# A hybrid decoder layer with 32 experts: another order of the expert steps, the last three of them scattered by products, the residual in the second step

## The chip, the cores and the metric

One Trainium2 chip; the kernel runs on 1 of its cores. The metric is the device time of one execution in microseconds (us). A core has a matmul engine (PE, with its weight loads PEld), a vector engine (DVE), a scalar engine (ACT), GpSimd (POOL) and SyncE (SP), which issues DMA transfers; ACT and POOL can issue transfers too. All transfers run on the same 16 DMA engines.

## The reference

One decoder layer on 512 tokens of 1024 values: attention in a window and a gated mixing stage, then a mixture of experts, each stage followed by a layer norm. The part that the change touches is the mixture:

```python
def routed_experts(x, w_router, b_router, w_gate_up, b_gate_up, w_down, b_down):
    top_val, top_idx = lax.top_k(logits, TOP_K)          # 4 of 32 experts for each token
    gates = jax.nn.softmax(top_val, axis=-1)
...
        h = clamped_swiglu(xb @ w_gate_up[e] + b_gate_up[e])
        y = (h @ w_down[e] + b_down[e]) * g[:, None]
        return acc.at[tok].add(y), None
...
h = layer_norm(DEEPNORM_ALPHA * h + ffn, ln2_g[l], ln2_b[l])
```

Each expert has 8 MB of gate and up weights and 4 MB of down weights, float32, so the 32 experts are 384 loads of 1 MB.

## The kernel before

The first part (to 240 us) is the attention and mixing stage, the router and the sort of the experts by the number of their tokens. Then the expert loop runs in steps, listed by the string `PLAN` (line 77). A letter is an expert: N and L are experts with up to 128 token places, X with up to 192, S with up to 64. A step is one word: `SS` is a pair of small experts that share the 128 rows of a tile and multiply at full float32 on two halves of the matmul array; `L` is one expert whose weights are first split by ACT (line 279) and DVE (line 280) into a high and a low part, three fast products for each block; `XS` is an expert of 192 places with a small one beside it, 128 rows twice, so it needs the products of two steps.

A step has an up phase (U; A and B for the two halves of XS) and a down phase (D0 and D1). The order is: up of step i, then down of step i-1, then up of step i+1; where step i is XS, the down of step i-1 lies between A and B. So every stretch below can be named by its phases: 4A, 3D, 4B, 5U, 4D and so on. Weights stream in that order. SP issues one load of 1 MB at a time (lines 293, 296, 299) into a ring of 11 buffers (`NRING_A`, `NRING_B`, `NRING_C`: 3 + 5 + 3); a buffer is free again when PE has used it, in an L step when ACT and DVE have split it. A phase of a step takes: SS up 16 loads, SS down 8, L up 8, L down 4, XS A, B and down 8 each.

Side work is written as generators that are moved on by `pump`, one piece between two groups of products: first `urgent` (the activation), then `later` (the output of a step), then the list `side` in its order, each entry when it is due. `prep` gathers the tokens of a coming step (POOL, line 1399), `prep_t` transposes them. At the end of an up phase all of `side` but the scatters is drained.

What an expert yields goes one of two ways. Up to step `LATE` - 1, `rows_out` (from line 1671) scales the result on ACT and writes it to DRAM as rows (`yd`, line 1686, issued by ACT, 0.5 MB for 128 rows). From step `LATE` on, `output` splits the result into two parts in two `sg` tiles (ACT line 1662, DVE line 1664) and `scatter` brings it to its tokens with 16 products (line 1414) and 8 additions (line 1416). The rows come back with `combine`: 16 gathers by POOL (line 1734) of 128 rows of 4 KB each, into tiles that are no longer needed; `combined` adds them to the residual stream (16 additions, line 1743). `combine` is put on `side` by `outputs(LATE - 1)`, `combined` at the end of the down phase of `LATE`. `residual` (8 products of line 1368, 8 additions of line 1371) starts the stream with the scaled input and the down biases; it runs in step 0.

`ending` (from line 1868) drains what is left on `side`, does the last half of the last down phase with loads by column halves (line 1892), places the last pair by products (line 1884) and normalises. In `side`, a scatter is put at the head; the additions of line 1743 to a token tile come after the scatter's additions to it.

```python
    seq = [(0, "A"), (0, "B"), (0, "D0"), (0, "D1")]
    for i in range(1, NS):
        down = [(i - 1, "D0"), (i - 1, "D1")] if i > 1 else []
        seq += [(i, "A")] + down + [(i, "B")] if wide(i) else [(i, "U")] + down
```

Of the kernel before, what the change touches and what calls it, by code (L numbers as in the profile page):

```python
# [73 lines left out]
R2L = R2 - R2H  # L74
PIF = 3.1415925

PLAN = "N SS L SS XS SS L L SS L L SS XS SS L L SS L L SS SS"


@with_exitstack  # L80
def kernel(ctx: ExitStack, tc: tile.TileContext, x, pos, gb_in, w_in, b_in, sinks,
                      gn_g, gn_b, w_sT, b_sT, w_out, b_out, ln1_g, ln1_b, w_router, b_router,
                      w_gu, b_gu, w_dn, b_dn, ln2_g, ln2_b, out, plan=PLAN):
    nc = tc.nc
# [22 lines left out]
    def ps_m():  # L107
        return ps[0].tile([P, 512], F32, name="misc", bufs=2)
# [105 lines left out]
    NS = len(steps)  # L214
# [19 lines left out]
        return [(steps[i][1].index(r), slice(q * n, q * n + n)) for q, (r, _) in enumerate(u)]  # L234


    LATE = NS - 2
    room = lambda r: P if r == 0 else 192 if r <= nx else P if r < nx + nl else 64
    late_ranks = [r for _, rs in steps[LATE:] for r in rs]
    first_row = [sum(room(q) for q in range(r) if q not in late_ranks) for r in range(E + 1)]  # L240
# [97 lines left out]
    with ExitStack() as pc:  # L338
# [667 lines left out]
        Q, L = {}, {}  # L1006
# [288 lines left out]
    def drain(g):  # L1295
        for _ in g:
            pass
# [21 lines left out]
    def tables():  # L1319
        pg = ps_m()  # L1320
        for t in range(T):
            nc.tensor.transpose(pg[:, t * P:(t + 1) * P], tabf[:, t].rearrange("p a e -> p (a e)"), ident)
        nc.vector.tensor_copy(trt, pg)
        yield
        pg = ps_m()
        for t in range(T):
            nc.tensor.matmul(pg[:, t * 3 * E:(t + 1) * 3 * E], lhsT=trt[:, t * P:(t + 1) * P],
                             rhs=pm3.rearrange("p a e -> p (a e)"), start=True, stop=True)
        pv = pg[:, 0:3 * T * E].rearrange("p (t j e) -> p j t e", j=3, t=T)
        nc.vector.tensor_copy(vpos, pv[:, 2])  # L1330
        for j in range(2):
            nc.vector.tensor_copy(aux[:, :, :, 1 + j], pv[:, j])
        yield

        capr = mw.tile([P, E], F32, name="capr", bufs=1)
        nc.gpsimd.memset(capr, 64.0)
        nc.gpsimd.memset(capr[:, 0:1 + nx + nl - 1], 128.0)
        if nx:
            nc.gpsimd.memset(capr[:, 1:1 + nx], 192.0)
        gover = mw.tile([P, T, E], F32, name="hT", bufs=HTB)  # L1340
        nc.vector.tensor_tensor(gover, vpos, capr[:, None, :].to_broadcast([P, T, E]), op=OP.is_gt)
        ovs = mw.tile([P, E], F32, name="capr2", bufs=1)
        nc.vector.reduce_sum(ovs, gover.rearrange("p t e -> p e t"), axis=AX.X)
        pg = ps_m()
        nc.tensor.matmul(pg[0:1, 0:E], lhsT=onec, rhs=ovs, start=True, stop=True)
        nc.vector.tensor_copy(over[:, 0:E], pg[0:1, 0:E])
        ovt = mw.tile([1, 1], F32, name="ovt", bufs=1)
        nc.vector.reduce_sum(ovt, pg[0:1, 0:E], axis=AX.X)
        nc.vector.tensor_copy(over[:, E:E + 1], ovt)
        gsum = rt.tile([P, T, E], F32, name="oh")  # L1350
        nc.gpsimd.tensor_add(gsum, aux.bitcast(F32)[:, :, :, 1], aux.bitcast(F32)[:, :, :, 2])
        nc.gpsimd.tensor_mul(gover, gover, gsum)
        nc.gpsimd.dma_start(out=god, in_=gover)
        yield
# [2 lines left out]
    for j in range(3):  # L1357
        nc.scalar.dma_start(out=braw[j * E:(j + 1) * E], in_=b_dn[0])

    def residual():  # L1360

        bdn = msplit.tile([P, 2, 512], F32R, name="hi").rearrange("p a b -> p (a b)")[0:3 * E]
        nc.scalar.copy(out=bdn, in_=braw)
        nc.vector.tensor_sub(bdn[E:E2], braw[E:E2], bdn[E:E2])
        for t in range(T):
            for c in range(2):
                pg = ps_m()
                nc.tensor.matmul(pg, lhsT=trt[0:3 * E, t * P:(t + 1) * P], rhs=bdn[:, c * 512:(c + 1) * 512],
                                 start=True, stop=True)
                h = hn[:, t, c * 512:(c + 1) * 512]  # L1370
                nc.vector.scalar_tensor_tensor(h, h, ALPHA, pg, op0=OP.mult, op1=OP.add)
                yield
# [46 lines left out]
    side = []  # L1419
# [3 lines left out]
    urgent, later = [], []  # L1423
# [49 lines left out]
    def slots0():  # L1473

        pa0 = ps_m()
        for t in range(T):
            nc.tensor.matmul(pa0[:, 0:2], lhsT=oh0[:, t], rhs=aux0[:, t], start=t == 0, stop=t == T - 1)
        SL[u0] = mw.tile([P, 4], F32, name="sl", bufs=6 + AHEAD)
        nc.vector.tensor_copy(SL[u0][:, 0:2], pa0[:, 0:2])
        yield  # L1480
# [3 lines left out]
    zrow = mw.tile([P, 2, 512], F32, name="y")  # L1484
    nc.gpsimd.memset(zrow[0:1], 0.0)
    nc.gpsimd.dma_start(out=yd[first_row[E]:first_row[E] + 1], in_=zrow[0:1].rearrange("p c j -> p (c j)"))
    side += [[slots0(), 2], [tables(), 0], [residual(), 0]]
    state = {}

    def begin(i):  # L1490
# [175 lines left out]
    def y_tile(u):  # L1666
        settle(1)
        YH[u] = [mw.tile([P, 2, 512], F32R, name="sg") for _ in range(2)]
        return YH[u]

    def rows_out(u, a):

        y = mw.tile([P, 2, 512], F32, name="y")
        gcol = SL[u][:, 1:2]
        for c in range(2):
            nc.scalar.activation(y[:, c], a[:, c], AF.Copy, scale=gcol)  # L1676
            yield
        n = P // len(u)
        if len(u) == 2 and u[0][1] == u[1][1] == 0:
            blocks = [(u[0], P)]  # L1680
        else:
            blocks = [(ro, n) for ro in u]
        p = 0
        for (r, off), m in blocks:
            row = first_row[r] + off
            nc.scalar.dma_start(out=yd[row:row + m], in_=y[p:p + m].rearrange("p c j -> p (c j)"))
            p += m
# [34 lines left out]
    def combine():  # L1722

        for n in range(4 * T):
            t, j = divmod(n, 4)
            if n < 4:
                g = mw.tile([P, KT, P], F32, name="xT", bufs=XTB).rearrange("p k s -> p (k s)")
            elif n < 6:
                g = mw.tile([P, D], F32, name="xg", bufs=AHEAD)
            elif n < 8:  # L1730
                g = mw.tile([P, 2, 512], F32, name="y").rearrange("p c j -> p (c j)")
            else:
                g = msplit.tile([P, 2, 512], F32, name="hi" if n % 2 else "lo").rearrange("p c j -> p (c j)")
            nc.gpsimd.indirect_dma_start(out=g, out_offset=None, in_=yd,
                                         in_offset=bass.IndirectOffsetOnAxis(ap=yrow[:, t, j:j + 1], axis=0))
            gathered.append((t, g))
            yield
# [3 lines left out]
    def combined():  # L1741
        for t, g in gathered:
            nc.vector.tensor_add(hn[:, t], hn[:, t], g)
            yield

    def outputs(i):
        if i < LATE:
            for u, a in zip(state[i]["us"], state[i]["dn"]):
                yield from rows_out(u, a)
                yield  # L1750
            if i == LATE - 1:
                side.append([combine(), 0])
            return
        for u, a in zip(state[i]["us"], state[i]["dn"]):
            y = y_tile(u)
            for c in range(2):
                yield from output(u, a[:, c:c + 1], y, slice(c, c + 1))
                yield
            scat.append([scatter(u), 0])
            side.insert(0, scat[-1])  # L1760
# [149 lines left out]
    with in_order():  # L1910
        before_ = None
        for i, ph in seq:
            if ph in ("U", "A"):
                begin(i)
                plan_prep(i)
            if i == NS - 1 and ph == "D1":
                break
            if ph in ("U", "A", "B") and before_ and before_[1] == "D1" and not wide(before_[0]):
                flush(urgent)
            elif ph != "D1":  # L1920
                flush()
            if ph == "U":
                phase_up(i)
            elif ph in ("A", "B"):
                phase_half(i, int(ph == "B"))
            else:
                phase_down(i, int(ph == "D1"))
            before_ = i, ph
            if i == 0:
                flush()  # L1930
            if i == LATE - 2 and ph in ("U", "A"):
                side.append([combine_rows(), 0])
            if (ph == "U" or ph == "B" and i or ph == "D1" and not i) and i < NS - 1:
                for ent in [e for e in side if e not in scat]:
                    side.remove(ent)
                    drain(ent[0])
            if ph == "D1":
                later.append(outputs(i))
                if i == LATE:
                    side.append([combined(), 0])  # L1940
                state.pop(i - 1, None)
        flush()
    ending()
# [112 lines left out]
```

## Time and profile before

| | us |
|---|---|
| device time, median of 3 runs | 1352.46 (1348.05 to 1354.04) |
| device time of the profiled execution | 1352.4 |
| its span, first to last instruction | 1350.2 |
| attention, mixing, router | 0 to 240 |
| expert loop | 240 to 1305 |
| last additions, last placing, layer norm, store | 1305 to 1350 |
| PE busy, share of the span | 91% |
| DVE busy | 47% |
| ACT busy | 32% |
| POOL busy | 14% |
| moved by DMA | 454.89 MB |

The profile is read by stretches, since its shares are means over stages with different limits. A stretch in which the transfers run at some 420 GB/s is limited by them; one in which PE is busy throughout and the transfers run slower is limited by PE.

### The profile page before, as it was taken

Reading aid. Unit: us, or ns where it says so; the run is one execution under the profiler, and the core shown is the slowest. Engines: PE = TensorE matmul, PEld = TensorE weight load, DVE = VectorE, ACT = ScalarE, POOL = GpSimd, SP = SyncE. Lnnn points to the kernel's source line nnn. Section 1 sums busy time; section 2 is a strip of 40 time slices with the busy share of each in tenths; the row PEclk is TensorE's granted clock in tenths of the full one; section 3 lists DMA queues with packets and bytes.
Section 4 is the critical chain, followed back from the end, with each engine's and each line's share of the span. In section 5 each row is a group of like instructions: output and inputs, shape, how many; then the busy total and the mean of one; then the engine's idle time right before and its main releaser. Section 6 shows DMA issues by size and latency. Waiting matters only on the chain.

```text
span 1350.2 us, 15317 instructions
## 1 busy us (share of the span) xinstructions
PE 1235.1 (91%) x5416; PEld 693.0 (51%) x5417; DVE 632.3 (47%) x1125; ACT 431.1 (32%) x623; POOL 194.9 (14%) x269
## 2 busy tenths in 40 slices
PE   5789899999998999999999999999999999997762
PEld 4767778444545333467476635333665477442220
DVE  7747767514404012268286632022565578330176
ACT  3335443103303101347174422101544356230002
POOL 5634735100001000000000010000000000003004
PEclk8889999999998999999999999999999999998895
DMA  7210185489999899999999999999999999999951
GB/s 248 79 63 32 63 270 189 152 309 420 420 421 413 314 415 415 379 422 419 378 420 421 420 419 416 361 403 421 389 420 377 403 421 422 417 421 418 417 205 65
DMA packets 85080, 454.89 MB, mean 337 GB/s; under 512 B 10813, under 2 KB 11861, under 8 KB 41476
## 3 DMA queue, kind: packets, MB, share of 16 engines
q1 hardware_dynamic: 75508, 423.76, 78.0%
q0 software_dynamic: 5536, 16.58, 3.2%
q10 hardware_dynamic: 3952, 13.51, 2.6%
q8 instruction: 44, 0.72, 0.2%
q14 instruction: 40, 0.33, 0.1%
HBM read 441.96 MB, written 15.27 MB: 339 GB/s over the span
## 4 chain that ended last, share of the span: by engine, by line
PE 73%; DMA 12%; DVE 9%; ACT 2%; issue 2%; POOL 1%; SPq 0%; ACTq 0%; POOLq 0%; DVEq 0%; another core or an unknown queue 0%
PE acc L1471 36%; PE acc L1465 7%; PE acc L1464 7%; PE acc L1467 7%; DMA raw<-in_w_dn_dram 7%; DMA raw<-in_w_gu_dram 5%; PE accA L427 2%; PE accA L428 2%; PE accA L429 2%; PE misc L1527 2%; DVE lo L280 1%; PE misc L1287 1%; ACT hi L279 1%; PE acc L1583 1%; PE misc L1386 1%
## 5 line engine op out<-in xcount | busy, mean ns | idle before, releaser
L1471 PE MATMUL acc<-raw,xT 128*64 128x512 f32 (+1 forms) x1600 | 414.5, 603 | 9.0 <-DMA raw<-in_w_gu_dram 6.6
L280 DVE TENSOR_TENSOR lo<-raw,hi 128x1024 fp32r<-128x1024 f32 x216 | 255.8, 1222 | 158.6 <-ACT hi L279 157.6
L1471 PEld LDWEIGHTS acc<-raw,xT 128*64 128x64 f32 (+1 forms) x1600 | 135.1, 144 | 237.7 <-issue 219.4
L279 ACT CAST hi<-raw 128x1024 fp32r<-128x1024 f32 x216 | 218.0, 1047 | 117.4 <-DMA raw<-in_w_gu_dram 42.1
L1471 PE MATMUL acc<-raw,hT 128*64 128x512 f32 (+1 forms) x768 | 199.1, 606 | 12.6 <-DMA raw<-in_w_dn_dram 11.8
L1399 POOL DMA_INDIRECT xg<-h1d,idx x22 | 23.9, 1085 | 827.7 <-DVE sl L1396 294.5
L1471 PEld LDWEIGHTS acc<-raw,hT 128*64 128x64 f32 (+1 forms) x768 | 65.8, 145 | 138.8 <-issue 118.6
L1464 PE MATMUL acc<-hi,xT 128*128 128x512 f32 x288 | 117.5, 408 | 0.0
L1465 PE MATMUL acc<-lo,xT 128*128 128x512 f32 x288 | 113.9, 396 | 0.0
L1467 PE MATMUL acc<-hi,xT 128*128 128x512 f32 x288 | 90.6, 396 | 0.0
L427 PE MATMUL accA<-hi,tT 128*128 128x512 f32 x152 | 66.4, 437 | 1.3 <-ACT tT L465 1.3
L1541 ACT ACTIVATE sg<-sg 128x512 f32<-128x512 f32 x38 | 24.0, 631 | 132.9 <-DVE sg L1540 132.9
L1464 PE MATMUL acc<-hi,hT 128*128 128x512 f32 x144 | 61.9, 430 | 4.0 <-ACT hi L279 4.0
L1465 PE MATMUL acc<-lo,hT 128*128 128x512 f32 x144 | 61.4, 427 | 4.0 <-DVE lo L280 4.0
L1392 DVE COPY sl<-misc 64x4 f32<-64x4 f32 (+1 forms) x33 | 5.3, 160 | 126.0 <-PE misc L1386 125.8
L428 PE MATMUL accA<-lo,tT 128*128 128x512 f32 x152 | 62.7, 413 | 0.0
L429 PE MATMUL accA<-hi,tT 128*128 128x512 f32 x152 | 62.3, 410 | 0.0
L1464 PEld LDWEIGHTS acc<-hi,xT 128*128 128x128 f32 x288 | 54.3, 189 | 14.2 <-issue 2.8
L1467 PEld LDWEIGHTS acc<-hi,xT 128*128 128x128 f32 x288 | 54.0, 188 | 13.0
L1465 PEld LDWEIGHTS acc<-lo,xT 128*128 128x128 f32 x288 | 54.2, 188 | 11.3
L1676 ACT ACTIVATE y<-acc,sl 128x512 f32<-128x512 f32 x42 | 27.2, 683 | 94.3 <-PE acc L1471 58.5
L1531 ACT COPY hT<-misc 128x512 f32<-128x512 f32 x28 | 16.4, 586 | 116.0 <-PE misc L1527 115.2
(409 smaller groups left out, 1390.6 us busy)
## 6 DMA issues: line engine op xcount, KB each, us to landing
raw<-in_w_gu_dram SPq DMA_DIRECT2D x248, 1024.0 KB, 14.0
raw<-in_w_dn_dram SPq DMA_DIRECT2D x124, 1024.0 KB, 14.9
yd<-y ACTq DMA_DIRECT2D x19, 512.0 KB, 8.0
raw<-in_w_gu_dram SPq DMA_DIRECT2D x16, 512.0 KB, 9.0
raw<-in_w_in_dram SPq DMA_DIRECT2D x7, 1024.0 KB, 13.3
raw<-in_w_out_dram SPq DMA_DIRECT2D x4, 1024.0 KB, 4.9
raw<-in_w_dn_dram SPq DMA_DIRECT2D x8, 512.0 KB, 23.9
hn<-in_x_dram SPq DMA_DIRECT2D x4, 512.0 KB, 10.9
```

The lines of the kernel that those rows point to most:

```text
L279: nc.scalar.copy(out=hi, in_=w.raw[:, 2 * h:2 * h + 2])
L280: nc.vector.tensor_sub(lo, w.raw[:, 2 * h:2 * h + 2], hi)
L427: nc.tensor.matmul(o, lhsT=a, rhs=hi, start=first, stop=False)
L428: nc.tensor.matmul(o, lhsT=a, rhs=lo, start=False, stop=False)
L429: nc.tensor.matmul(o, lhsT=b, rhs=hi, start=False, stop=last)
L1464: nc.tensor.matmul(outs[g], lhsT=lhs[0], rhs=hi[:, g], start=first, stop=False)
L1465: nc.tensor.matmul(outs[g], lhsT=lhs[0], rhs=lo[:, g], start=False, stop=False)
L1467: nc.tensor.matmul(outs[g], lhsT=lhs[1], rhs=hi[:, g], start=False, stop=last)
L1471: nc.tensor.matmul(outs[g][cs], lhsT=lhs[0][:, cs], rhs=ws[m].raw[:, 2 * q + g], start=first, stop=last)
L1527: nc.tensor.transpose(pt[:, j * P:(j + 1) * P], pick(act, j), ident)
L1541: nc.scalar.activation(g[:, 0], g[:, 0], AF.Gelu_apprx_sigmoid)
L1676: nc.scalar.activation(y[:, c], a[:, c], AF.Copy, scale=gcol)
```

## The change

Four edits. The plan has the same letters in another order: steps 5 to 20 were `SS L L SS L L SS XS SS L L SS L L SS SS` and become `L SS L L SS XS L L SS L L SS L SS SS SS`. `LATE` becomes `NS - 3`: the steps 18, 19 and 20 are scattered by products and step 17 is the last to write rows. `combine` is put on `side` behind the up phase of step `LATE + 1`, ahead of the down phase of step 18, and `combined` ahead of the output of step 18. `residual` is cut in two: `table_down` (the split of the down biases) stays in step 0, the products and additions are put on `side` at the end of step 0 and run in the up phase of step 1.

```diff
--- before.py
+++ after.py
@@ -74,7 +74,7 @@
 R2L = R2 - R2H
 PIF = 3.1415925
 
-PLAN = "N SS L SS XS SS L L SS L L SS XS SS L L SS L L SS SS"
+PLAN = "N SS L SS XS L SS L L SS XS L L SS L L SS L SS SS SS"
 
 
 @with_exitstack
@@ -234,7 +234,7 @@
         return [(steps[i][1].index(r), slice(q * n, q * n + n)) for q, (r, _) in enumerate(u)]
 
 
-    LATE = NS - 2
+    LATE = NS - 3
     room = lambda r: P if r == 0 else 192 if r <= nx else P if r < nx + nl else 64
     late_ranks = [r for _, rs in steps[LATE:] for r in rs]
     first_row = [sum(room(q) for q in range(r) if q not in late_ranks) for r in range(E + 1)]
@@ -1357,11 +1357,19 @@
     for j in range(3):
         nc.scalar.dma_start(out=braw[j * E:(j + 1) * E], in_=b_dn[0])
 
-    def residual():
+    def table_down():
 
         bdn = msplit.tile([P, 2, 512], F32R, name="hi").rearrange("p a b -> p (a b)")[0:3 * E]
         nc.scalar.copy(out=bdn, in_=braw)
         nc.vector.tensor_sub(bdn[E:E2], braw[E:E2], bdn[E:E2])
+        bdns.append(bdn)
+        yield
+
+    bdns = []
+
+    def residual():
+
+        bdn = bdns[0]
         for t in range(T):
             for c in range(2):
                 pg = ps_m()
@@ -1484,7 +1492,7 @@
     zrow = mw.tile([P, 2, 512], F32, name="y")
     nc.gpsimd.memset(zrow[0:1], 0.0)
     nc.gpsimd.dma_start(out=yd[first_row[E]:first_row[E] + 1], in_=zrow[0:1].rearrange("p c j -> p (c j)"))
-    side += [[slots0(), 2], [tables(), 0], [residual(), 0]]
+    side += [[slots0(), 2], [tables(), 0], [table_down(), 0]]
     state = {}
 
     def begin(i):
@@ -1748,8 +1756,6 @@
             for u, a in zip(state[i]["us"], state[i]["dn"]):
                 yield from rows_out(u, a)
                 yield
-            if i == LATE - 1:
-                side.append([combine(), 0])
             return
         for u, a in zip(state[i]["us"], state[i]["dn"]):
             y = y_tile(u)
@@ -1934,10 +1940,14 @@
                 for ent in [e for e in side if e not in scat]:
                     side.remove(ent)
                     drain(ent[0])
+            if (i, ph) == (LATE + 1, "U"):
+                side.append([combine(), 0])
             if ph == "D1":
-                later.append(outputs(i))
                 if i == LATE:
                     side.append([combined(), 0])
+                later.append(outputs(i))
+                if i == 0:
+                    side.append([residual(), 0])
                 state.pop(i - 1, None)
         flush()
     ending()
```

## Rows read from the trace of the kernel before

**Rows 1.** The page's 40 slices of 33.8 us: granted clock, transfers, GB/s.

```profile
PEclk8889999999998999999999999999999999998895
...
DMA  7210185489999899999999999999999999999951
...
GB/s 248 79 63 32 63 270 189 152 309 420 420 421 413 314 415 415 379 422 419 378 420 421 420 419 416 361 403 421 389 420 377 403 421 422 417 421 418 417 205 65
```

**Rows 2.** Stretches: us, busy us by engine (instructions), PEclk, DMA share, GB/s.

```profile
240.10:296.80 56.70, 52.94 (x160) 25.69 (x158) 19.78 (x69) 5.73 (x10) 5.38 (x9) 0.97 0.65 230
...
428.40:503.70 75.30, 75.30 (x285) 28.11 (x284) 6.01 (x10) 5.93 (x9) 1.31 (x2) 1.00 0.94 372
...
536.50:566.00 29.50, 29.50 (x102) 10.28 (x100) 7.86 (x9) 6.99 (x9) 0.00 (x0) 1.00 1.01 421
...
566.00:590.80 24.80, 24.80 (x120) 20.32 (x118) 15.97 (x18) 14.90 (x18) 0.00 (x0) 1.00 0.91 366
...
605.30:646.10 40.80, 37.76 (x172) 29.50 (x170) 30.36 (x37) 24.84 (x30) 1.46 (x2) 1.00 1.01 420
...
646.10:820.70 174.60, 169.23 (x766) 99.19 (x764) 98.32 (x154) 75.92 (x92) 8.70 (x13) 0.98 1.00 411
...
820.70:896.10 75.40, 75.40 (x287) 28.16 (x286) 6.05 (x10) 6.01 (x9) 1.31 (x2) 1.00 0.98 393
...
896.10:1062.30 166.20, 163.17 (x724) 85.60 (x724) 73.56 (x110) 58.21 (x72) 4.35 (x7) 1.00 0.98 399
...
1062.30:1208.60 146.30, 142.33 (x636) 87.74 (x632) 90.79 (x117) 71.36 (x83) 4.54 (x19) 0.98 1.01 420
...
1227.40:1288.50 61.10, 42.45 (x140) 12.29 (x137) 5.77 (x9) 3.71 (x6) 8.00 (x9) 0.89 1.02 416
...
1305.00:1350.20 45.20, 8.45 (x17) 4.05 (x16) 33.39 (x67) 9.15 (x19) 13.94 (x27) 0.59 0.13 48
```

**Rows 3.** The waits of the SP queue: us in total, times, longest.

```profile
SPq L296 <- PE acc L1471: 180.0, 61, 6.4
...
SPq L296 <- DMA yd<-y: 124.9, 12, 14.0
```

**Rows 4.** Timeline of PE: start, us, instruction [idle before <-what ended it].

```profile
1230.80 5.35 PE L1471 MATMUL acc<-raw,xT 128*64 128x512 f32 x16 [2.34 <-issue]
...
1238.34 5.28 PE L1471 MATMUL acc<-raw,xT 128*64 128x512 f32 x16 [2.18 <-DMA raw<-in_w_gu_dram]
...
1283.56 3.65 PE L1471 MATMUL acc<-raw,hT 128*64 128x512 f32 x16 [2.19 <-DMA raw<-in_w_dn_dram]
...
1288.55 3.65 PE L1471 MATMUL acc<-raw,hT 128*64 128x512 f32 x14 [1.34 <-DMA raw<-in_w_dn_dram]
```

**Rows 5.** Groups by line: busy us, mean ns, idle before them.

```profile
L1368 PE MATMUL misc<-hi,sh 96*128 96x512 f32 x8 | 4.4, 610 | 0.6 <-DVE hn L1371 0.6
...
L1414 PE MATMUL misc<-sg,sh 128*128 128x512 f32 x16 | 4.8, 421 | 0.0
...
L1416 DVE TENSOR_TENSOR hn<-hn,misc 128x512 f32<-128x512 f32 x8 | 5.1, 683 | 9.4 <-PE misc L1414 9.4
```

**Rows 6.** Timeline of POOL: first and last of 16 gathers of rows.

```profile
1217.97 1.01 POOL L1734 DMA_INDIRECT xT<-yd,yrow  x1 [106.50 <-DMA yd<-y]
...
1254.29 0.94 POOL L1734 DMA_INDIRECT hi<-yd,yrow  x1 [2.67 <-DMA raw<-in_w_dn_dram]
```

**Rows 7.** Timelines of DVE and PE behind the loop: additions and placing.

```profile
1302.21 1.22 DVE L1743 TENSOR_TENSOR hn<-hn,xT 128x1024 f32<-128x1024 f32 x1
...
1313.57 0.48 DVE L1876 TENSOR_SCALAR sh<-itok,sl 128x512 fp32r<-128x512 f16 x1
...
1317.50 1.22 DVE L1743 TENSOR_TENSOR hn<-hn,hi 128x1024 f32<-128x1024 f32 x1
...
1314.19 0.77 PE L1884 MATMUL misc<-sg,sh 128*128 128x512 f32 x1 [9.17 <-DVE sh L1876]
```

**Rows 8.** Timeline of ACT: a wait for the first down load of step 10.

```profile
799.14 1.99 ACT L279 CAST hi<-raw 128x1024 fp32r<-128x1024 f32 x2 [7.09 <-DMA raw<-in_w_dn_dram]
```

## The prediction

> **What bounds the kernel now.** I read the slices first: from 300 us to the end of the loop the transfers run at some 420 GB/s with dips, and only the first 300 us and the last 45 are outside of it [rows 1]. So the loop is the 384 loads of weights at 1.0486 MB / 421 GB/s = 2.49 us each, plus whatever time the transfers idle. The stretches say why they idle [rows 2]: with XS in it, 4A to 4B, PE is busy for all of 75.3 us and the transfers run at 372 GB/s; with L up behind an XS down (566 to 591) PE is busy throughout at 366. There PE is the limit, and the ring of 11 loads is full, so SP waits for PE (180 us in all [rows 3]). Behind 1062 us the rate is 420 up to the end and PE waits instead: a pair of loads lands, PE takes 3.65 us for it and waits 2.19 us for the next [rows 4]. The loss of the transfers against 421 GB/s, length x (1 - rate/421), is 8.8 us in 4A to 4B, 3.2 in 6U, 4.1 in 8U to 10D, 5.0 in 12A to 12B and 8.7 in 13U to 17U, some 30 us in all, beside the start (230 GB/s in step 0, where N holds the ring) [rows 2].
>
> The view to keep: the loop ends when the last load lands, and every us in which the ring is full and the transfers stand still is lost for good, wherever it lies. The reader is to ask of an order of steps not how much PE or DMA time it has (all orders have the same) but whether PE's long steps come in a row.
>
> **The residual.** In step 0 PE spends 4.4 us on the 8 products of line 1368 [rows 5], and step 0 is where the loads wait for PE. Taken out, the loads of the next steps are released 4.4 us sooner. In the up phase of step 1 the same 8 products and additions come back; PE uses up its 4.4 us there, but that phase only frees buffers whose loads still queue behind others, so I cost it at nothing. Bounds: 0 gained (if step 1 gives it all back) to 4.4. I take 4.4, since the transfers reach their full rate within step 1 [rows 1]. The split biases hold one of four `hi` buffers until then, so the fourth early split of step 2 on ACT waits for the last residual product, about 3 us, with the step's activation behind it on ACT and DVE; neither is needed before 1D.
>
> **The third scattered pair.** Step 18 adds 16 products (4.8 us of PE), 8 additions (5.1 us of DVE) [rows 5] and takes away one write of 0.52 MB, 1.25 us of transfer. They lie in 20U and 19D, where PE waits over 2 us for each pair of loads [rows 4], so the products cost nothing; without that cover, 4.8. A wait is added: the two `sg` tiles for step 18 are free only after step 19's transposes, in the third and fourth group of 20U. Queued behind on ACT is the copy of those transposes, on DVE nothing that PE needs before 19D. Step 20's activation then waits for the last product of step 18's scatter, early in 19D; it is wanted in 20D. Nothing, at most one group of products (3.65 us [rows 4]). SP waits for the landing of such a write before a load goes out, 10 us each time (124.9 us in 12 waits [rows 3]); where the queue is full that is free, and the write that goes lay there.
>
> **The gathers sooner.** Now the first starts at 1217.97, released by a write of rows, the last at 1254.29 [rows 6]. They move by about one down phase. All are 8.39 MB, 19.9 us of transfer, and they take it from the loads wherever they lie while the transfers are full: a pair then lands every 7.5 us instead of 5 (1230.80 to 1238.34 and 1283.56 to 1288.55, starts [rows 4]). Moved within a full stretch, they cost and save nothing. What would save is the additions leaving the tail: 12 of them run from 1302 to 1318 and hold the last placing, whose PE waited 9.17 us for `sh` [rows 7]. But counting pumps, I get 8 gathers issued in 18D, one in 20U, two in 19D, one in 20D0 (scatters go first, and 19D1 has its transposes): `combined` stands behind `combine` and starts only when `ending` drains, behind step 19's scatter, as now. I cost the tail at no change; between 0 and -9.2.
>
> **The order.** The phases that follow each other in the new plan nearly all have a twin in the trace, so I lay twins end to end; step 4 and all ahead of it is the same. (1) 4A starts at 428.4 - 4.4 = 424.0. (2) 4A, 3D, 4B as now, 75.3: 5U at 499.3. (3) 5U is now L, 24.8, and 4D 29.5 with PE full in both [rows 2]: 6U at 553.6. (4) 6U to 8D are SS up, L down, L up, SS down, L up, L down, SS up, L down: the same row as 8U to 10D now, 174.6; I add 2.0, since step 4's two groups of rows are written at its head and SP waits for them: 10A at 730.2. (5) 10A, 9D, 10B as 12A to 12B, 75.4: 11U at 805.6. (6) 11U L up 24.8, 10D 29.5, 12U and 11D as 7U and 6D, 40.8: 13U at 900.7. (7) 13U to 15D is again the row 8U to 10D; there the first load of 10D lands at 799.14 [rows 8], 153.0 behind the start: 15D's first load lands at 1053.7. (8) From there the ring is no limit any more. Up to the second pair of 20D0 there are 3 + 8 + 8 + 16 + 4 + 16 + 8 + 16 + 8 + 4 = 91 loads, 226.6 us, with 16 gathers, 3 row writes and 1 token gather of 0.52 MB each, 24.9 us: 1305.2. Now that pair lands at 1288.55 [rows 4]. So the loop ends 16.7 us later.
>
> A check by the same count on the kernel before: from 799.14 there are 175 loads and 34 transfers of 0.52 MB, 478.1 us, plus losses of 5.0 and 8.7, 1291 against 1288.55. It is good to 3 us.
>
> What happens there: steps 10 to 12 put XS, L, L together. From 10A to 11D PE needs 170.5 us for 52 loads, which take 129.5 us and some 9 of rows and tokens. The ring can be 27 us ahead (11 loads), and SP stands still for the rest. The three pairs at the end want that time back (24 loads, 60 us, against some 45 of PE for a pair), but then it is gone. The tail (1305 to 1350) and its state are as now: span 1350.2 + 16.7 = 1366.9, and with the 2.2 us around it **1369.1 us**. The profiled time, 1352.4, is that of the median, 1352.46.
>
> **A rule weighed.** In the stretch with the gathers the granted clock is 0.89 on average between its two levels, 1.2 and 2.4 GHz [rows 2], and a pair of loads takes PE 5.28 us instead of 3.65 [rows 4]. The Trainium skill, "TensorE: Matmul & The Clock Gate", section "HAM oscillation — how this bites in real kernels", says that a matmul engine which waits for transfers between its batches falls back to the low clock and starts each batch slow. It speaks against this change, since three pairs at the end mean more such waits. By that rule, the trace agrees for the stretch with gathers; for 1283 to 1292 it doesn't, the pairs there take 3.65.
>
> **The rivals.** (a) The transfers do not stand still in the middle: PE gets through 10A to 11D in 145 us or less, or the lead is large enough. Then only the residual and the write remain, -4.4 - 1.2, 1346.8, not slower. For: the total work is the same, and 30 us of idle now is something that an order can win. Against: PE is full in every twin [rows 2]; the point is the 170.5 us, and XS and L have no slack in them. (b) The additions leave the tail: some pump more than I count, or `ending` places them sooner; 9.2 us less [rows 7], 1359.9. (c) The low clock stays: from 18D to 20D0 some 20 pairs without gathers take 5.28 us each [rows 4] where their loads take 4.98, 6 us: 1375. Against: the pairs at 1283.56 and 1288.55. (d) The residual only moves its cost: 1373.5.
>
> **How the numbers follow.** Forecast 0.60 (1361 to 1376, from 3 us of the count, 4 of pieces (3) and (6), which have no twin as a whole, and 2 of piece (4)); (a) 0.12; (b) 0.12; (c) and (d) 0.16. The range goes from 1350, which leaves out most of (a), to 1380: 0.8. Faster than 0.5% (6.8 us, about what a measurement of this kernel can tell from no change) asks for (a) and (b) together, or more of the 30 us: 0.10. Within: most of (a), half of (b): 0.14. Slower 0.76.
>
> **What would show it.** Right: 10D to 11D at 340 to 380 GB/s with PE full, 13U at about 901, SP's waits for PE well over 180 us, and from 1054 on 420 GB/s with PE waiting from 18D. Wrong: no dip behind 10A; 4A not at 424; the additions of line 1743 ahead of the last loads; pairs at 5.3 us in 20U. The forecast falls if PE's twins shrink, above all if L behind XS takes less than 24.8.

## Result: slower by 1.7%, and the profile after

The changed kernel takes 1374.3 us (median of 4 runs, 1372.87 to 1377.68) against 1353.25 for the kernel before beside it: a ratio of 1.0168, 95% interval 1.0146 to 1.0189. Forecast were 1369.1 and a range of 1350 to 1380. The profiled execution took 1377.68 (span 1376.0), the longest of the four.

The slices of the changed kernel's page (40 of 34.4 us each; they answer [rows 1]):

```profile
PEclk9989999999998999999999999999999999999995
GB/s 245 75 61 31 71 260 185 200 325 422 383 387 406 354 416 317 365 420 422 420 410 405 378 415 276 398 348 420 418 420 382 421 370 423 421 418 418 421 216 64
```

The dips to 317 and to 276 are new, and so are 383 and 387 from 344 to 413 us. The stretches show what they are (length, busy time of each engine, granted clock, DMA share, GB/s; they answer [rows 2]):

```profile
core 0: us, PE busy (x) PEld busy (x) DVE busy (x) ACT busy (x) POOL busy (x), PEclk, DMA share, GB/s
430.90:506.30 75.40, 75.40 (x286) 28.17 (x285) 12.95 (x20) 9.98 (x13) 1.43 (x3) 1.00 0.98 390
532.00:561.40 29.40, 29.40 (x103) 10.17 (x102) 4.47 (x11) 3.06 (x5) 1.45 (x2) 1.00 0.71 271
735.70:811.00 75.30, 75.30 (x285) 28.12 (x284) 13.65 (x25) 9.93 (x13) 1.31 (x2) 1.00 1.00 400
811.00:907.00 96.00, 93.98 (x395) 61.94 (x393) 57.42 (x72) 46.48 (x55) 3.04 (x5) 0.98 0.88 349
1062.80:1173.00 110.20, 98.28 (x432) 55.54 (x432) 52.77 (x75) 38.68 (x48) 4.63 (x22) 0.97 0.98 406
1173.00:1211.00 38.00, 32.97 (x148) 11.55 (x148) 0.02 (x1) 3.52 (x6) 2.86 (x3) 1.00 1.01 420
1211.00:1239.00 28.00, 20.06 (x68) 5.67 (x66) 3.85 (x6) 1.26 (x2) 12.66 (x13) 0.88 1.02 418
1239.00:1289.00 50.00, 41.48 (x152) 14.91 (x150) 4.79 (x8) 2.33 (x4) 0.00 (x0) 0.97 1.02 419
```

The dips to 317 and 276 are where L stands behind XS: 4D behind 5U (532 to 561) and 11U to 12U with 10D and 11D (811 to 907). PE is busy for 29.40 of 29.40 us and 93.98 of 96.00 there, and the transfers run at 271 and 349 GB/s: for the rest of the time they stand still because no buffer comes free. From 1173 on the rate is full and PE waits. SP's waits, in us, times and longest, agree (answering [rows 3]; line 299 waited 13.9 us in 12 times for these splits before):

```profile
SPq L296 <- PE acc L1479: 193.0, 60, 9.7
SPq L296 <- DMA yd<-y: 105.8, 13, 12.0
SPq L299 <- DVE lo L280: 60.0, 24, 9.3
```

Two waits are longer than the prediction had them, and one has stayed. The first is ahead of 2U: ACT, then PE (start, length, engine, line, operation; in brackets the idle time before it and what ended it):

```profile
321.56 1.05 ACT L279 CAST hi<-raw 128x1024 fp32r<-128x1024 f32 x1 [0.49 <-DMA raw<-in_w_gu_dram]
328.73 1.05 ACT L279 CAST hi<-raw 128x1024 fp32r<-128x1024 f32 x1 [6.12 <-PE misc L1376]
332.27 0.63 ACT L1549 ACTIVATE sg<-sg 128x512 f32<-128x512 f32 x1 [2.49 <-DVE sg L1548]
332.98 0.79 PE L1591 MATMUL acc<-bt,sel 64*128 64x512 f32 x2 [3.85 <-DVE sg L1551]
```

The early splits are those of the next L step's first loads, queued ahead of its phase. The fourth (328.73) stood on ACT for 6.12 us until the last residual product had read the biases' buffer. DVE's half of that split and step 1's activation are queued behind it, and 2U's second accumulator is one that this activation has to empty: PE waited 3.85 us. The second is in 15D1; the one that has stayed is in the tail:

```profile
1068.29 0.29 DVE L1713 TENSOR_TENSOR hT<-vpos,capr 128x128 f32<-128x128 f32 x1 [3.30 <-PE acc L1473]
1070.61 0.69 DVE L1548 TENSOR_SCALAR sg<-acc 128x512 f32<-128x512 f32 x1
1073.87 3.87 ACT L279 CAST hi<-raw 128x1024 fp32r<-128x1024 f32 x4
1074.94 0.79 PE L1472 MATMUL acc<-hi,hT 128*128 128x512 f32 x1 [6.29 <-ACT hi L279]
1338.06 1.22 DVE L1751 TENSOR_TENSOR hn<-hn,lo 128x1024 f32<-128x1024 f32 x1
1339.19 0.48 DVE L1882 TENSOR_SCALAR sh<-itok,sl 128x512 fp32r<-128x512 f16 x1
1339.82 0.76 PE L1890 MATMUL misc<-sg,sh 128*128 128x512 f32 x1 [9.18 <-DVE sh L1882]
```

L1713 is the first operation of the table of rows to gather (`combine_rows`). It comes in step LATE - 2, so in step 16 instead of 17, it needs an `hT` tile that PE still reads, and step 16's activation waits behind it on DVE. 15D's splits wait behind the activation on ACT, and PE stands still for 6.29 us. In the tail nothing has changed: the wait of 9.18 us for `sh` is the 9.17 of [rows 7].

### The profile page after: what moved, and what is told of

It reads as the page before. It is cut to its first block, busy times and chain, and to the rows that moved or that the text cites. A ratio compares the mean times of both kernels' runs of the same rounds, so it can differ in the third digit from the quotient of the medians.

```text
span 1376.0 us, 15351 instructions
## 1 busy us (share of the span) xinstructions
PE 1247.8 (91%) x5432; PEld 703.4 (51%) x5433; DVE 640.3 (47%) x1136; ACT 431.2 (31%) x623; POOL 195.0 (14%) x271
## 5 line engine op out<-in xcount | busy, mean ns | idle before, releaser
L1407 POOL DMA_INDIRECT xg<-h1d,idx x22 | 23.9, 1087 | 825.6 <-DVE sg L1548 282.8
L1479 PEld LDWEIGHTS acc<-raw,hT 128*64 128x64 f32 (+1 forms) x768 | 69.3, 145 | 132.0 <-issue 108.1
L1292 DVE TENSOR_TENSOR xT<-misc,xT 128x512 fp32r<-128x512 f32 x18 | 12.4, 691 | 136.9 <-ACT xT L1290 136.5
L1473 PEld LDWEIGHTS acc<-lo,xT 128*128 128x128 f32 x288 | 54.8, 190 | 11.2
L1541 DVE TENSOR_TENSOR hT<-misc,hT 128x512 fp32r<-128x512 f32 x18 | 12.4, 692 | 94.1 <-ACT hT L1539 94.1
## 6 DMA issues: line engine op xcount, KB each, us to landing
raw<-in_w_dn_dram SPq DMA_DIRECT2D x8, 512.0 KB, 15.9
```

The costliest lines, as they stand in the source:

```text
L1407: nc.gpsimd.indirect_dma_start(out=xg, out_offset=None, in_=h1d, in_offset=bass.IndirectOffsetOnAxis(ap=idx[:, :1], axis=0), bounds_check= ...
L1473: nc.tensor.matmul(outs[g], lhsT=lhs[0], rhs=lo[:, g], start=False, stop=False)
L1479: nc.tensor.matmul(outs[g][cs], lhsT=lhs[0][:, cs], rhs=ws[m].raw[:, 2 * q + g], start=first, stop=last)
```

## Experiments

All were run beside the kernel before, whose median in the three groups was 1351.5, 1349.6 and 1351.7 us. Ratios are to it, with 95% intervals; a difference called "by the ratios" is a difference of two of them times 1351.5 us, and where runs of two groups are compared, it is the safer one.

### The order alone, and each other part alone

**order_alone**, the kernel before with only the new order:

```diff
-PLAN = "N SS L SS XS SS L L SS L L SS XS SS L L SS L L SS SS"
+PLAN = "N SS L SS XS L SS L L SS XS L L SS L L SS L SS SS SS"
```

> The kernel before with the new order of steps and nothing else: the residual in step 0, two scattered steps, the gathers where they were. Theory 1 (the order alone costs the time, the residual's move gains nothing): slower by all of the 21 us, 1372 to 1376, with the transfers down to 340 to 360 GB/s behind 10A. Theory 2 (the order costs 16.7 as in the prediction, and the third scattered pair or the sooner gathers cost the other 4.4): 1368 to 1371.

Measured: 1370.36 us, ratio 1.0154 (1.0131 to 1.0177), that is 17.7 to 23.9 us. The order is nearly the whole result. The transfers ran at 341 GB/s from 811 to 907, where 340 to 360 were expected. The median lies in the bounds of theory 2 and the ratio's middle (1372.3 us) in those of theory 1, so this run doesn't part them; the next ones do. Theory 2 also misread the prediction: its 16.7 us held the residual's -4.4, so the order alone stood in it at 21.1.

**residual_alone**, the kernel before with `table_down` in step 0 and the products of `residual` in step 1:

```diff
-    side += [[slots0(), 2], [tables(), 0], [residual(), 0]]
+    side += [[slots0(), 2], [tables(), 0], [table_down(), 0]]
...
+                if i == 0:
+                    side.append([residual(), 0])
```

> The kernel before with only the residual moved from step 0 into step 1's up phase. Theory of the prediction: the loads are released 4.4 us sooner and it stays so, 1349. Rival, from the trace of the changed kernel: the fourth early split of step 2 stands on ACT until the last residual product has read the biases' buffer, step 1's activation stands behind it on ACT and DVE, and 2U's second accumulator waits for that activation; 2U then starts some 4 us later and the gain is used up, 1352 to 1354, with PE waiting 3 to 4 us for DVE ahead of 2U where it waits 1.0 now.

Measured: 1352.29, ratio 1.0010 (0.9995 to 1.0025). The 4.4 us are not there. In its trace PE waits 3.85 us ahead of 2U, as in the changed kernel.

**residual_unblocked**, the same with the buffer counted as used while the residual reads it:

```diff
         bdns.append(bdn)
+        unused[0] += 1
         yield
...
+                if (t, c) == (T - 1, 1):
+                    unused[0] -= 1
                 yield
```

> As residual_alone, but while the split biases hold a buffer of the weights' splits, that buffer is counted as used, so the fourth split of step 2 is queued only behind the last residual product and step 1's activation does not stand behind it. If the queued split is what gives the gain back: PE's wait ahead of 2U is back to 1 us, and 1348 to 1350. If the eight products and additions give it back simply by lying in step 1: as residual_alone, 1352 to 1354.

Measured: 1348.87, ratio 0.9985 (0.9972 to 0.9997): 3.4 us under residual_alone. Its ACT and PE at the same place:

```profile
327.51 0.63 ACT L1552 ACTIVATE sg<-sg 128x512 f32<-128x512 f32 x1 [7.66 <-DVE sg L1551]
328.22 0.50 PE L1594 MATMUL acc<-bt,sel 64*128 64x512 f32 x2 [1.64 <-DVE sg L1554]
```

No split is left ahead of the activation, and PE waits 1.64 us and not 3.85 (1 us was expected). So the queued split cost 3.4 us. What remains of the move is a gain of 2.0 us by the ratio (0.4 to 3.8), not the 4.4 of the prediction; whether the 8 products take the rest by lying in step 1 is not shown.

**order_undone**, the changed kernel with the order of before (the `PLAN` line above, reversed):

> The changed kernel with the order of before, all else as changed: residual in step 1, three scattered steps (the third is then the L of step 18) and gathers begun a step ahead. If the order alone makes the difference: as residual_alone within 2 us, 1351 to 1355. If the third scattered step or the sooner gathers cost something too: 1356 to 1360.

Measured: 1358.15, ratio 1.0059 (1.0039 to 1.0079). The order makes most of the difference, but something else costs 5.9 us over residual_alone. Its trace has the 6.29 us wait of PE for ACT's split in 15D1 again. That gave the next pair.

### The table of rows

**order_undone_table_later** and **changed_table_later**, both with one line:

```diff
-            if i == LATE - 2 and ph in ("U", "A"):
+            if i == LATE - 1 and ph in ("U", "A"):
                 side.append([combine_rows(), 0])
```

> order_undone with one line changed: the table of the rows to gather (9 small DVE operations that write into hT tiles) is made in step 17 again and not in step 16. If it is the table that costs order_undone its 6 us (DVE waits for an hT tile, step 16's activation stands behind the table on DVE, the splits of 15D behind the activation on ACT, and PE stands still for 6.3 us): as residual_alone, 1350 to 1354. If the third scattered step or the gathers cost it: 1356 to 1360 as order_undone.

> The changed kernel with the same one line: the table made in step 17. There the same stall of PE, 6.29 us at 15D1, stands where the transfers run at 406 GB/s and lose 3.8 us. If the stall is paid in full: 6 us less, 1367 to 1369. If only the transfers' loss counts: 2 to 4 us less, 1370 to 1372. If it is hidden: 1373 to 1376.

Measured: 1349.26, ratio 0.9976 (0.9957 to 0.9996), 8.9 us under order_undone by the medians; and 1369.03, ratio 1.0129 (1.0104 to 1.0154), 5.3 us under the changed kernel, at the edge of what "paid in full" would give. So the table in step 16 cost: 5.3 us in the changed kernel (some 1 to 10 by the ratios' intervals), 8.9 in order_undone (11.2 by the ratios). order_undone_table_later comes out 0.7 us under the range of its first theory. PE in 15D1 of changed_table_later, and the 50 us behind it there and in the changed kernel:

```profile
1063.10 0.50 PE L1472 MATMUL acc<-hi,hT 128*128 128x512 f32 x1 [0.84 <-ACT hi L279]
1080.00:1130.00 50.00, 50.00 (x231) 25.25 (x231) 18.11 (x41) 13.25 (x18) 2.87 (x19) 1.00 1.01 421
```

```profile
1090.00:1140.00 50.00, 50.00 (x238) 26.34 (x238) 18.48 (x31) 15.46 (x21) 2.08 (x5) 1.00 0.94 387
```

The stall itself is followed by a full ring: at 387 GB/s instead of 421 the transfers lose 50 x (1 - 387/421) = 4.0 us. PE's clock fell as well: the granted clock is 0.51 from 1074.9 to 1080, behind the 6.29 us without work, and 1.00 from 1080 to 1090.

With the table back, the third scattered step and the sooner gathers cost nothing: order_undone_table_later lies 3.0 us under residual_alone by the medians (4.6 by the ratios, whose intervals touch). Whether they gain is not settled: the two loops in the traces are as long to within 1 us, and so are the tails, and three of the twelve runs of order_undone_table_later (1343 to 1344) carry much of the difference.

### Where the order costs

**pairs_two_at_end**, the kernel before with an order that differs from the new one only behind step 16:

```diff
-PLAN = "N SS L SS XS SS L L SS L L SS XS SS L L SS L L SS SS"
+PLAN = "N SS L SS XS L SS L L SS XS L L SS L L SS SS L SS SS"
```

> The kernel before with an order that is the new one up to step 16 (XS, L, L together in steps 10 to 12) but ends L, SS, SS as before: only steps 17 and 18 of the new order are exchanged. Theory 1 (the time is lost where XS, L, L stand together and the ring is full; behind 15D the transfers are full whatever the order is): as order_alone, 1367 to 1374. Theory 2 (three pairs at the end are what costs, since PE waits for their loads): back to the kernel before, 1350 to 1356.

Measured: 1369.01, ratio 1.0144 (1.0114 to 1.0173), as order_alone. The third pair at the end is worth nothing that these runs can tell, in either direction; the time is lost before it. Three stretches of the kernel before, then order_alone, then pairs_two_at_end:

```profile
505.00:735.00 230.00, 226.58 (x1012) 126.30 (x1009) 119.18 (x168) 95.67 (x115) 8.03 (x12) 1.00 0.99 407
735.00:905.00 170.00, 165.01 (x686) 80.96 (x686) 58.04 (x105) 42.64 (x55) 6.33 (x10) 0.98 1.00 404
905.00:1060.00 155.00, 151.97 (x668) 81.39 (x666) 67.62 (x90) 57.14 (x70) 4.35 (x7) 1.00 0.98 401
```

```profile
505.00:735.00 230.00, 226.24 (x988) 131.16 (x988) 116.12 (x172) 93.21 (x113) 9.26 (x14) 0.98 0.97 393
735.00:905.00 170.00, 167.98 (x690) 88.80 (x688) 71.06 (x96) 56.82 (x68) 4.35 (x7) 1.00 0.93 367
905.00:1060.00 155.00, 152.34 (x698) 88.47 (x695) 90.38 (x135) 68.70 (x81) 6.75 (x10) 0.99 0.99 409
```

```profile
505.00:735.00 230.00, 224.76 (x991) 129.22 (x991) 116.48 (x172) 93.23 (x114) 9.27 (x14) 0.99 0.97 394
735.00:905.00 170.00, 167.98 (x688) 88.80 (x686) 71.06 (x96) 56.88 (x68) 4.35 (x7) 1.00 0.93 369
```

By length x (1 - rate/421) the transfers stand still for 7.6 + 6.9 + 7.4 = 21.9 us before and 15.3 + 21.8 + 4.4 = 41.5 in order_alone. The difference, 19.6 us, lies in the interval of the order's cost, 17.7 to 23.9. In these single traces the loop, from its first product to the second pair of 20D0, is 15.9 us longer (241.3 to 1305.6 against 240.1 to 1288.6).

**pairs_three_spread**, three pairs at the end and a pair behind each XS:

```diff
-PLAN = "N SS L SS XS SS L L SS L L SS XS SS L L SS L L SS SS"
+PLAN = "N L SS L L SS L L SS L L SS XS SS L L SS XS SS SS SS"
```

> The kernel before with an order that ends SS, SS, SS but has a pair behind each XS and no three long steps in a row: N L SS L L SS L L SS L L SS XS SS L L SS XS SS SS SS. Theory 1 (only XS, L, L in a row costs): within 8 us of before, 1345 to 1360. Theory 2 (three pairs at the end cost): 1366 to 1375.

Measured: 1361.21, ratio 1.0084 (1.0053 to 1.0116), a miss for both. The first and last of these stretches in its trace, behind them those of the kernel before:

```profile
300.00:430.00 130.00, 128.34 (x588) 81.70 (x587) 83.85 (x110) 67.29 (x78) 4.35 (x7) 0.99 0.96 394
1060.00:1210.00 150.00, 143.96 (x591) 50.55 (x588) 12.66 (x16) 12.79 (x22) 0.41 (x2) 1.00 0.97 398
```

```profile
300.00:430.00 130.00, 121.55 (x530) 63.59 (x527) 50.63 (x96) 36.99 (x46) 6.70 (x11) 0.97 1.01 416
1060.00:1210.00 150.00, 146.03 (x652) 89.10 (x650) 92.22 (x126) 72.04 (x84) 4.54 (x19) 0.98 1.01 420
```

Its transfers lose 8.3 us in the first (L straight behind N) and 8.2 in the last (XS late), where the kernel before loses 1.5 and 0.4. Between them, from 430 to 1060, it loses 23.7 us by the same count, the kernel before 31.0: a pair behind each XS does pay there. So the loss isn't tied to XS, L, L in a row; in this trace it lies where L stands straight behind N and where XS comes late. The sum, 7.4 us, agrees with the loop, which is 7.0 us longer (242.0 to 1297.4); the runs are 11.3 us longer by the ratio. How much three pairs at the end cost in the best order stays open.

### The tail

**additions_sooner**, the kernel before:

```diff
             if i == LATE - 1:
-                side.append([combine(), 0])
+                drain(combine())
+                side.append([combined(), 0])
...
-                if i == LATE:
-                    side.append([combined(), 0])
```

> The kernel before with the 16 gathers issued in one go when step 18's rows are written and their additions pumped from then on, so that they stand ahead of step 19's scatter on DVE and not behind it. If the additions hold the last placing, as the 9.17 us of PE's wait for sh say: 1341 to 1344. If they only push DVE's other work (step 20's activation, step 19's scatter) back: 1348 to 1354.

Measured: 1339.39, ratio 0.9915 (0.9883 to 0.9946), 10.2 us less by the medians and a little more than the first theory gave. The last placing waits 0.77 us where it waited 9.17 [rows 7]:

```profile
1308.61 0.50 PE L1885 MATMUL misc<-sg,sh 128*128 128x512 f32 x1 [0.77 <-ACT sg L1662]
```

**changed_additions_sooner**, the changed kernel:

```diff
             if (i, ph) == (LATE + 1, "U"):
-                side.append([combine(), 0])
+                drain(combine())
...
                 if i == LATE:
-                    side.append([combined(), 0])
+                    drain(combined())
```

> The changed kernel with the gathers issued in one go behind 19U and all 16 additions ahead of step 18's output on DVE, where DVE waited until 1268 anyway. If they leave the tail for good: 1363 to 1367, with the loop's end where it is. If the last gathers land too late and the additions hold step 18's output, and with it 20U: 1372 to 1378.

Measured: 1361.75, ratio 1.0092 (1.0062 to 1.0123), 12.6 us under the changed kernel by the medians, 10.3 by the ratios; the median is 1.3 us below the first range. DVE and PE there:

```profile
1260.20 1.22 DVE L1751 TENSOR_TENSOR hn<-hn,lo 128x1024 f32<-128x1024 f32 x1 [3.66 <-DMA lo<-yd,yrow]
1263.95 1.23 DVE L1751 TENSOR_TENSOR hn<-hn,hi 128x1024 f32<-128x1024 f32 x1 [2.53 <-DMA hi<-yd,yrow]
1265.56 0.75 DVE L1672 SCALAR_TENSOR_TENSOR sg<-acc,sl,sg 128x512 fp32r<-128x512 f32 x1 [0.38 <-PE misc L1535]
1324.01 0.49 PE L1890 MATMUL misc<-sg,sh 128*128 128x512 f32 x1 [0.77 <-ACT sg L1670]
```

The last addition ends as step 18's output becomes free to start, and the last placing waits 0.77 us, for ACT, and not 9.18 for `sh`. From the second pair of 20D0 to the end, this kernel's trace takes 50.0 us (1310.2 to 1360.2), the changed kernel's 61.8: the gain lies in the tail.

### All repairs together

**both_repairs**: residual_unblocked and additions_sooner in the kernel before, its order kept. **changed_repaired**: the changed kernel and its order with the split, the table and the additions repaired as above.

> The kernel before, order unchanged, with the residual moved as in residual_unblocked and the additions as in additions_sooner. If the two gains add (one lies in steps 0 to 2, the other in the tail): 1351.5 - 2 - 10, so 1336 to 1341. If the sooner loop gives the gathers less cover: 1341 to 1348.

> The changed kernel, its order kept, with all three repairs: the fourth split not queued, the table in step 17, the additions ahead of step 18's output. If what then remains above both_repairs is the order: 18 to 21 us above it, 1355 to 1361. If the repairs overlap: 1361 to 1365.

Measured: 1336.9, ratio 0.9890 (0.9866 to 0.9914), the lowest median of the study (its interval overlaps that of additions_sooner); and 1353.71, ratio 1.0017 (1.0001 to 1.0032), 16.8 us above it and below what was expected (17.2 by the ratios). That is what the order costs when nothing else is in the way, less what the third scattered step may give.

## Why the prediction was right, and where it was not

The forecast was 1369.1, the result 1374.3. Against before, 16.7 us were forecast and 21.1 measured by the medians (22.7 by the ratio). By parts, from ratios times 1351.5 us:

| part | forecast, us | measured, us |
|---|---|---|
| order | +21.1 (its 16.7 held the residual's -4.4) | +20.8 (17.7 to 23.9) |
| residual moved | -4.4 | +1.4 (-0.7 to +3.4) |
| table of rows in step 16 | not priced | +5.3 (1.0168 - 1.0129), some +1 to +10 |
| third scattered step, sooner gathers | 0 | -4.6 (0.9976 - 1.0010), some -8 to -1; not found in the traces |
| sum | +16.7 | +22.9, and 22.7 measured |

The sum closes because the order costs as much with the other edits as alone once the table is back in step 17: 20.7 us between order_undone_table_later and changed_table_later. Between order_undone and the changed kernel it is 14.7, since the table cost the old order more. That the total came within 6 us is in part luck: the table's +5.3 and the -4.6 of the last part were both unforeseen and nearly cancel.

**The order: right, by its mechanism and its size.** The dips are at the places that were named, 349 GB/s from 811 to 907 against 340 to 380 forecast, with PE all but full, and the twins hold: 75.40 and 75.30 us for the stretches with XS against 75.3 and 75.4 forecast [rows 2], 29.40 for 4D against 29.5. The size is 21.1 forecast against 20.8 by the ratio, 18.8 by the medians and 15.9 in the traces. The loop began 3.4 us later in this execution (first product at 243.5, before at 240.1). Measured from there, 13U came 2.9 us later than forecast and 15D's first load 1.3 us later. Two details were wrong. "PE is full in every twin" doesn't hold for 7U with 6D, where PE was busy for 37.76 of 40.80 us at 420 GB/s [rows 2]. And SP's waits for PE were to be "well over 180"; they are 193.0, and the waits of line 299 for the splits on DVE rose from 13.9 to 60.0: read as the same full ring, under another name.

**The residual: wrong.** The prediction saw the wait, "the fourth early split of step 2 on ACT waits for the last residual product, about 3 us, with the step's activation behind it on ACT and DVE", and then priced it at nothing with "neither is needed before 1D". That is the step that failed: the activation also empties the accumulators, and 2U needs them at once. 4A came 3.5 us later than forecast, counted from the loop's start; single traces differ by about as much there (4A at 188.2 us behind the start before and at 185.3 in order_alone, whose steps up to 4A are the same), so residual_alone against residual_unblocked is the better evidence. The wait becomes lost time where the ring is full behind it: the stretch from 2U's start, before and changed,

```profile
328.50:370.00 41.50, 41.50 (x197) 25.86 (x196) 22.21 (x36) 17.30 (x21) 1.55 (x2) 1.00 1.01 419
333.70:375.50 41.80, 41.80 (x188) 26.92 (x186) 21.92 (x35) 16.55 (x20) 1.56 (x2) 0.93 0.97 390
```

with PE busy throughout in both. From 330 to 430 us the rate is 388 GB/s in residual_alone and 412 in residual_unblocked. The wait also cost clock (stretches of the changed kernel around it):

```profile
329.00:333.00 4.00, 0.15 (x4) 0.05 (x2) 3.08 (x5) 1.41 (x2) 0.00 (x0) 0.92 1.02 424
333.00:339.00 6.00, 6.00 (x15) 4.30 (x16) 3.73 (x5) 1.67 (x2) 0.00 (x0) 0.50 1.02 422
339.00:345.00 6.00, 6.00 (x31) 4.99 (x30) 2.84 (x4) 4.53 (x6) 0.00 (x0) 0.98 1.01 419
```

After 3.85 us without work the granted clock is 0.50, the lower level (1.2 GHz), for the next 6 us, in which PE does 15 matmuls, and 31 in the 6 us behind them: half of 6 us, an estimate of 3, is lost on top of the wait. Behind the 1.64 us of residual_unblocked the clock is 1.00, the upper level (2.4 GHz):

```profile
328.00:334.00 6.00, 5.78 (x27) 4.61 (x28) 5.25 (x8) 4.47 (x7) 0.00 (x0) 1.00 1.01 419
```

The rule of the Trainium skill that the prediction weighed ("TensorE: Matmul & The Clock Gate", section "HAM oscillation — how this bites in real kernels": a wait for data between batches makes the next batch start cold) agrees with the trace here as far as the cold start goes: 0.50 behind the wait. The wait itself was for an accumulator and not for data, and the prediction looked for such waits only at the end of the loop.

**The table: missed.** The prediction counted the gathers that `LATE` moves, and not `combine_rows`, which hangs on `LATE` as well. Each thing placed by the changed constant has to be listed, and for the moved one who stands behind it on DVE.

**The last part.** From 15D's first load to the second pair of 20D0, 251.5 us were forecast and 255.8 passed:

```profile
1058.40 1.99 ACT L279 CAST hi<-raw 128x1024 fp32r<-128x1024 f32 x2 [6.07 <-DMA raw<-in_w_dn_dram]
1314.17 3.65 PE L1479 MATMUL acc<-raw,hT 128*64 128x512 f32 x14 [1.20 <-DMA raw<-in_w_dn_dram]
```

The 4.0 us lost behind the table's stall are nearly all of the difference. The claim that the ring is no limit from there was wrong for that reason: without the stall, in order_alone and changed_table_later, the rate is 420 to 422 GB/s from 1060 to 1210.

**The third scattered step and the gathers: right within their bounds.** They cost nothing; the gain of 4.6 us in the table is not explained. The products of line 1422 lie in 20U and 19D beside pairs that land every 5 us, DVE waits for step 19's transposes until 1268 and nobody waits for that, and the additions stay in the tail as counted.

**The rivals.** (a), no standing still, fell with the dips. (b), the additions leave the tail, did not happen by itself; its price of 9.2 us was about right (10.2 and 12.6 by the medians when it was made to happen, 11.5 and 10.3 by the ratios). (c), the low clock at the end, fell: the first pairs of 20U, beside the last gathers, still took 4.83 to 5.34 us (1240.97 to 1256.01; the granted clock is 0.93 from 1239 to 1263), the prediction's sign "pairs at 5.3 us in 20U", but from 1263 to 1289 it is 1.00, and pairs without other products beside them take 3.65. (d), the residual only moves its cost, came true.

## What to carry to other kernels

Where a ring of loads covers an uneven sequence of steps, lay measured twins of the steps end to end and charge each microsecond in which the ring is full: here time of PE-bound steps in a row was lost, and DMA-bound steps gathered at the end did not bring it back. Price a helper's wait by everything queued behind it on its in-order engine, down to the accumulators that it empties. When a constant moves one piece of work, list every other piece that is placed by it.

## What the runs showed of the hardware that was not expected

The wait of 3.85 us ahead of 2U cost PE an estimated 3 us of clock beside the wait itself, and the 6.29 us in 15D1 were followed by 5 us at 0.51. The start of the loop, behind code that the experiments don't touch, came at 239.1 us (residual_alone), 240.1 (before), 243.5 (changed) and 246.9 (additions_sooner) in the profiled executions, for a reason that no run shows, so single executions are to be compared from the loop's start on.
